# Modulation products in column strips and a first projection that runs inner chunk by inner chunk

## The chip, the cores and the metric

One core of one Trainium2 chip runs the whole program. The metric is device microseconds (us) of one execution; three executions of the kernel before gave 1886.78, 1886.98 and 1887.4, and the median, 1886.98 us, is the time before.

## The reference, cut to what matters

One layer of an encoder is applied to two token streams, x_prompt (1024 tokens) and x_sample (512 tokens), each of width 1024, with the same weights. Each stream has one conditioning vector `c`, which is turned into six modulation vectors of width 1024:

```python
mod = (jnp.dot(jax.nn.silu(c), w_ada) + b_ada)[:, None, :]
sh1, sc1, gt1, sh2, sc2, gt2 = jnp.split(mod, N_MOD, axis=-1)

h = rms_norm(x, g_pre_mix) * (1.0 + sc1) + sh1
proj = jnp.dot(h, w_in)                      # q, k, v of 12 heads, and two gMLP inputs
...                                          # dilated attention in 3 groups, gMLP, concat
mix = jnp.dot(jnp.concatenate([attn, gm], axis=-1), w_out)
x = x + gt1 * rms_norm(mix, g_post_mix)

h = rms_norm(x, g_pre_ffn) * (1.0 + sc2) + sh2
gate, up = jnp.split(jnp.dot(h, w_gu), 2, axis=-1)
f = jnp.dot(jax.nn.silu(gate) * up, w_down)
return x + gt2 * rms_norm(f, g_post_ffn)
```

Nothing of the layer's main work can begin before `sh1` and `sc1` (modulations 0 and 1) are there, because they go into every `h`. The other four modulations are needed later: `gt1` when the first output projection is finished, `sh2` and `sc2` ahead of the FFN, `gt2` at its end.

## The kernel before

**Layout.** Tokens are cut into three groups of 512: groups 0 and 1 are x_prompt (class P, two halves), group 2 is x_sample (class S). Activations lie transposed, 128 channels on the partitions and 512 tokens along the row, in KC = 8 inner chunks. A large product is made by `mm3` (L158): per inner chunk three matmuls, high part by high part, high by low, low by high, with operands that `split` (L137) has cut in two (a ScalarE cast, then a subtraction on VectorE or GpSimd). One output tile of 128 columns for 512 tokens is thus 24 matmuls of 128x512.

**The planner.** The program is written as plain Python in an order; the framework (`schedule_with_timeline_sim=True`, L1054) then orders the instructions of each engine by its own estimate of the time line, with the program order as priority. Buffers belong to tags with a fixed count (`BUFS`, L103; `PBUFS`, L114). The tags that matter here are `tb` (2 buffers of 512 columns), `xc` (3), `h` (16), `wraw` (4), `whl` (4), `sc` (6) and the PSUM tags `st` (2 banks) and `mm` (4 banks).

**The start.** `run` (L937) begins with `ada_first` (L290), a generator of four steps, one per quarter of modulations 0 and 1. A step loads four 512 KB pieces of `w_ada` into `h` buffers and multiplies them with `silu(c)`: the two columns of `silu(c)` lie in a wide field of zeros in two `qk` buffers, and a window that slides over it by 32 columns puts four column blocks into one 128x128 result. That is 32 matmuls of 128x128 a step, each written as two instructions, so 256 instructions in all. VectorE then transposes the result into a `tb` tile and `finish_mod` (L280) adds the bias and makes G, which is (1 + sc1) * g_pre_mix. Between the steps `run` loads group 0, computes its row statistics (`x_stats`, L349, then `rms_now` and `spread`, which use `st` banks and one `tb` tile), loads the weights of two projection tiles (`FIRST_WIN`), and after the fourth step loads group 1. Then `make_h(0)` and `make_h(1)` run one after the other through `modulate` (L374), which makes one chunk of `h` from x: VectorE multiplies x by the row statistics into a `tb` tile (L380), ScalarE applies G and the shift in place (L382), ScalarE casts the high part (L138), and GpSimd (H01 = 'P') subtracts the low part (L139).

**The projections.** `attention_slot` (L680) goes over nine tiles of q, k and v; for class P each tile is made for both halves, by `project` (L407): the weights of a tile are loaded and split, all 24 matmuls of half 0 are issued, evacuated from PSUM, then those of half 1. For the first slot of P the first two tiles are projected together.

**The other modulations.** `ada_rest` (L318) is a generator that `more_ada` (L423) advances by a rate per projected tile, and `ffn` (L894) by one step per pair of hidden tiles. One step handles half of the inner dimension for one block of 512 columns of one modulation: four loads of 256 KB (three into `xc`, one into `tb`), four matmuls with a stationary operand of 32 columns (two real ones, 30 zeros; `silz`) that write to four strips of 32 partitions of one `st` bank, a ScalarE copy of the bank into a `tb` tile (L336), four matmuls with `sel` that add the strips and turn the result (L338), and a copy or an addition into `mod`. Each of these matmuls is written as two instructions. Four modulations times two blocks times two halves make 16 steps.

## Time and profile before

| | us |
|---|---|
| median of three executions | 1886.98 |
| the profiled execution | 1886.02 |
| its span, first to last instruction | 1884.2 |
| TensorE busy (matmul) in the span | 1846.7 |
| VectorE, ScalarE, GpSimd busy | 928.3, 690.6, 149.0 |
| mean granted share of the TensorE clock | 0.993 |

The profile shows one execution. TensorE's instructions appear on two rows, PE (matmul) and PEld (weight load), which overlap. "Idle before" is the time for which an engine waited, and the arrow names what ended the wait. The queue that issues transfers is SP. Times in the timeline count from the first instruction of the span.

### The profile page before, as it was taken

The page shows a single profiled execution, that of the slowest core. Times are in us where ns is not written, and L with a number is a line of the kernel's source. Part 1 is how long each engine was busy: PE and PEld are TensorE (multiplying, and loading weights), DVE is VectorE, ACT ScalarE, POOL GpSimd, SP SyncE. Part 2 cuts the span into 40 slices and gives each one's busy share as a digit, 9 for nine tenths or more (in the row PEclk, how much of TensorE's full clock was granted, in tenths as well). Part 3 has the DMA queues.
Part 4 walks back from the last instruction along what each step waited for, and adds up shares of the span by engine and source line. Part 5 has one row for each costly group of instructions (what it writes and reads, how often), then busy time and mean ns, then how long its engine had stood idle before and what let it go on. Part 6 is the DMA issues. An engine that isn't in the chain of part 4 may idle for free.

```text
span 1884.2 us, 23515 instructions
## 1 busy us (share of the span) xinstructions
PE 1846.7 (98%) x8866; PEld 1471.2 (78%) x8866; DVE 928.3 (49%) x1447; ACT 690.6 (37%) x1180; POOL 149.0 (8%) x102
## 2 busy tenths in 40 slices
PE   7999999999999999999999999999999999999997
PEld 7777876766777777878888888888888888888886
DVE  4334864473795467834443427444442374444223
ACT  3511642152444456533333423333342333333222
POOL 1400100010122012100000100000020000000001
PEclk9999999999999999999999999999999999999999
DMA  8112322234353367642223435322243342222432
GB/s 340 38 55 76 110 95 93 90 118 134 111 176 114 132 218 217 213 162 92 97 94 108 123 94 181 109 95 95 95 122 97 95 169 97 93 95 95 137 96 75
DMA packets 123682, 228.30 MB, mean 121 GB/s; under 512 B 13744, under 2 KB 19120, under 8 KB 123568
## 3 DMA queue, kind: packets, MB, share of 16 engines
q1 hardware_dynamic: 123424, 226.73, 36.2%
q8 instruction: 69, 1.13, 0.2%
q14 instruction: 45, 0.37, 0.1%
q10 hardware_dynamic: 144, 0.07, 0.0%
HBM read 206.30 MB, written 20.45 MB: 120 GB/s over the span
## 4 chain that ended last, share of the span: by engine, by line
PE 59%; DVE 0%; POOL 0%; DVEq 0%; ACT 0%; issue 0%
PE pmm L156 58%; PE pst L156 1%; DVE sc L861 0%; DVE sc L863 0%; POOL rq L216 0%; DVE whl L139 0%; DVEq L1054 0%; ACT tb L227 0%; DVE rq L215 0%
## 5 line engine op out<-in xcount | busy, mean ns | idle before, releaser
L156 PE MATMUL pmm<-h,whl 128*128 128x512 f32 x5772 | 1384.2, 398 | 11.7 <-ACT h L138 5.2
L156 PEld LDWEIGHTS pmm<-h,whl 128*128 128x128 f32 x5772 | 1079.1, 189 | 288.6 <-issue 22.6
L139 DVE TENSOR_TENSOR whl<-wraw,whl 128x512 fp32r<-128x512 f32 (+1 forms) x548 | 386.0, 707 | 461.3 <-ACT whl L138 458.1
L138 ACT CAST whl<-wraw 128x512 fp32r<-128x512 f32 (+1 forms) x548 | 333.2, 609 | 674.4 <-PE pmm L156 558.5
L139 POOL TENSOR_TENSOR h<-tb,h 128x512 fp32r<-128x512 f32 x40 | 59.6, 1497 | 554.9 <-ACT h L138 546.7
L156 PE MATMUL pmm<-qk,whl 128*128 128x512 f32 x414 | 100.0, 394 | 0.0
L908 DVE SCALAR_TENSOR_TENSOR ta<-ta,pmm 128x512 f32<-128x512 f32 x66 | 45.4, 687 | 110.8 <-ACT ta L907 110.7
L156 PEld LDWEIGHTS pmm<-qk,whl 128*128 128x128 f32 x414 | 77.8, 188 | 18.3
L907 ACT ACTIVATE ta<-pmm 128x512 f32<-128x512 f32 x66 | 39.5, 598 | 141.4 <-PE pmm L156 141.4
L909 DVE SCALAR_TENSOR_TENSOR ta<-ta,pmm 128x512 f32<-128x512 f32 x66 | 45.3, 687 | 79.2 <-PE pmm L156 79.0
L190 DVE TENSOR_TENSOR acc<-acc,ta 128x512 f32<-128x512 f32 x55 | 38.6, 702 | 55.4 <-ACT ta L807 44.3
L156 PE MATMUL pst<-qk 64*128 64x128 f32 (+3 forms) x384 | 61.7, 320 | 0.7 <-DVE st L782 0.7
L156 PEld LDWEIGHTS pst<-qk 64*128 64x128 f32 (+1 forms) x384 | 45.6, 187 | 20.1 <-issue 14.3
L216 POOL TENSOR_TENSOR rq<-rq,half 128x4 f32<-128x4 f32 (+1 forms) x11 | 11.7, 1068 | 526.6 <-DVE rq L215 521.9
L382 ACT ACTIVATE tb<-tb,mod,G 128x512 f32<-128x512 f32 x48 | 38.8, 815 | 39.8 <-DVE tb L380 36.0
L156 PE MATMUL pmm<-v,whl 128*128 128x512 f32 x207 | 51.4, 392 | 0.0
L139 POOL TENSOR_TENSOR h<-xc,h 128x512 fp32r<-128x512 f32 x24 | 33.7, 1414 | 171.3 <-ACT h L138 155.1
L806 ACT ACTIVATE sc<-pmm,G 128x512 f32<-128x512 f32 x47 | 32.2, 686 | 40.8 <-PE pmm L156 40.6
L156 PEld LDWEIGHTS pmm<-v,whl 128*128 128x128 f32 x207 | 38.8, 188 | 8.8
L460 DVE SCALAR_TENSOR_TENSOR sc<-cst,pst 128x512 f32<-128x512 f32 (+2 forms) x56 | 26.9, 512 | 37.8 <-PE pst L156 37.7
L620 POOL PARTITION_ALL_REDUCE st<-st x8 | 21.0, 2637 | 224.1 <-DVE st L556 224.1
L156 PE MATMUL pst<-h,qk 128*128 128x128 f32 x256 | 31.8, 286 | 7.0 <-DMA h<-in_wada 6.8
(163 smaller groups left out, 1299.6 us busy)
## 6 DMA issues: line engine op xcount, KB each, us to landing
wraw<-in_wgu SPq DMA_DIRECT2D x264, 256.0 KB, 2.7
wraw<-in_wdn SPq DMA_DIRECT2D x120, 256.0 KB, 2.6
wraw<-in_win SPq DMA_DIRECT2D x84, 256.0 KB, 2.8
xc<-in_wada SPq DMA_DIRECT2D x48, 256.0 KB, 3.7
wraw<-in_wout SPq DMA_DIRECT2D x48, 256.0 KB, 3.0
xc<-in_x SPq DMA_DIRECT2D x40, 256.0 KB, 3.6
xc<-x SPq DMA_DIRECT2D x40, 256.0 KB, 3.7
h<-in_wada SPq DMA_DIRECT2D x16, 512.0 KB, 9.6
```

Of the source, the lines that this page charges most:

```text
L138: self.nc.scalar.copy(hi, src)
L139: (eng or self.nc.vector).tensor_tensor(out=lo, in0=src, in1=hi.bitcast(F32), op=ALU.subtract)
L156: self.nc.tensor.matmul(out, lhsT, rhs, start=start, stop=stop, skip_group_check=True)
L190: nc.vector.tensor_tensor(out=acc, in0=acc, in1=t, op=ALU.add)
L216: nc.gpsimd.tensor_tensor(out=y, in0=y, in1=self.half8[:, :n], op=ALU.pow)
L382: nc.scalar.activation(t, t, AF.Identity, bias=sh[:, kc, c:c + 1], scale=G[:, kc, c:c + 1])
L460: self.nc.vector.scalar_tensor_tensor(out=out, in0=table, scalar=slope, in1=ps, op0=ALU.mult, op1=ALU.add)
L620: self.nc.gpsimd.partition_all_reduce(x[:, :grp.n], x[:, :grp.n], channels=128, reduce_op=RED.max)
L806: nc.scalar.activation(ys[-1][:, mt % 2], ps, AF.Copy, scale=G[:, mt, c:c + 1])
L907: nc.scalar.activation(t, ps[0], AF.Tanh, scale=0.5)
L908: nc.vector.scalar_tensor_tensor(out=t, in0=t, scalar=1.0, in1=ps[0], op0=ALU.add, op1=ALU.mult)
L909: nc.vector.scalar_tensor_tensor(out=t, in0=t, scalar=0.5, in1=ps[1], op0=ALU.mult, op1=ALU.mult)
```

## The change

- `ada_first` multiplies with `silz`: a stationary operand of 32 columns per inner chunk, eight matmuls of 128x512 a step, into four strips of one bank, inner chunks 4 to 7 added onto the strips of 0 to 3. A new helper `turned` copies the bank into a `tb` tile and adds and turns the strips with `sel`, as `ada_rest` did. The layout of the first two modulations' weights in memory changes with it, and the two columns of `sel` are loaded early by a transfer of their own.
- `ada_rest` makes one step out of two: eight loads, eight strip matmuls into one bank, one turn, one copy. The 16 steps become 8, and the rates at which they are called are halved (in `ffn`, every second pair).
- `run` issues group 0's load first, then the first step, group 0's statistics and group 1's load. The rest (three steps, group 1's statistics, `make_h`) moves into `start`, which is called inside the first attention slot behind the weight loads of four tiles.
- The first four tiles of P's first slot go through a new `project_first`: for half 0 the loop over inner chunks is the outer one, with the four tiles inside it and four `mm` banks open; half 1 follows tile by tile as before. The weights of the third and fourth of them lie in `sc` buffers.
- `make_h(0)` and `make_h(1)` are woven, chunk by chunk; the low part of half 0 is made on VectorE (H0 = 'V'), that of half 1 on GpSimd (H1 = 'P').

```diff
+    def turned(self, ps, n):
+        e = self.t2("tb")
+        self.nc.scalar.copy(e, ps)
+        for i in range(n):
+            self.mm(ps[:, 2 * i:2 * i + 2], e[:, 128 * i:128 * i + 128], self.sel, i == 0)
+        return ps[:, 0:2 * n]
+
     def ada_first(self):
-        z = []
-        for i in range(2):
-            t = self.t("qk", [128, 4, 256])
-            nc.vector.memset(t, 0.0)
-            nc.vector.tensor_copy(t[:, :, 96:98], self.sil[:, 4 * i:4 * i + 4])
-            z.append(t)
         for ch in range(4):
             ps = self.p("st")
             for pc in range(4):
-                w = self.t("h", [128, 2, 4, 128])
+                w = self.t("h", [128, 2, 512])
                 nc.sync.dma_start(out=w, in_=self.a["wada1"][ch, pc])
                 for k2 in range(2):
                     kc = 2 * pc + k2
-                    for q in range(4):
-                        self.mm(ps[:, 0:128], z[kc // 4][:, kc % 4, 96 - 32 * q:224 - 32 * q], w[:, k2, q],
-                                kc == 0 and q == 0, kc == 7 and q == 3)
-            tr = self.t2("tb")
-            nc.vector.transpose(out=tr[:, 0:128], in_=ps[:, 0:128])
+                    j = 32 * (kc % 4)
+                    self.mm(ps[j:j + 32], self.silz[:, kc], w[:, k2], kc < 4)
             ks = slice(2 * ch, 2 * ch + 2)
             nc.vector.tensor_copy(self.mod[:, 0:2, ks, :],
-                                  tr[:, 0:128].rearrange("p (m k i) -> p m k i", m=2, k=2)[:, :, :, 0:2])
+                                  self.turned(ps, 4).rearrange("p (m k i) -> p m k i", m=2, k=2))
             self.finish_mod(0, ks)
             self.finish_mod(1, ks)
             yield
 
     def ada_rest(self, ms):
         for m in ms:
             for blk in range(2):
                 ks = slice(4 * blk, 4 * blk + 4)
-                for hf in range(2):
-                    ws = []
-                    for j in range(4):
-                        w = self.t2("xc" if j < 3 else "tb")
-                        nc.sync.dma_start(out=w, in_=self.a["wada2"][m - 2, 4 * hf + j, :, 512 * blk:512 * blk + 512])
-                        ws.append(w)
-                    ps = self.p("st")
-                    for j in range(4):
-                        self.mm(ps[32 * j:32 * j + 32], self.silz[:, 4 * hf + j], ws[j], True)
-                    e = self.t2("tb")
-                    nc.scalar.copy(e, ps)
-                    for i in range(4):
-                        self.mm(ps[:, 2 * i:2 * i + 2], e[:, 128 * i:128 * i + 128], self.sel, i == 0)
-                    o = self.mod[:, m, ks]
-                    pv = v3(ps[:, 0:8], 2)
-                    if hf:
-                        nc.vector.tensor_tensor(out=o, in0=o, in1=pv, op=ALU.add)
-                    else:
-                        nc.vector.tensor_copy(o, pv)
-                    yield
+                ps = self.p("st")
+                for kc in range(KC):
+                    w = self.t2("tb" if kc % 4 == 3 else "xc")
+                    nc.sync.dma_start(out=w, in_=self.a["wada2"][m - 2, kc, :, 512 * blk:512 * blk + 512])
+                    j = 32 * (kc % 4)
+                    self.mm(ps[j:j + 32], self.silz[:, kc], w, kc < 4)
+                nc.vector.tensor_copy(self.mod[:, m, ks], v3(self.turned(ps, 4), 2))
                 self.finish_mod(m, ks)
+                yield
 
+    def project_first(self, grp, tiles, steps):
+        ws = []
+        for i, (ti, _, _) in enumerate(tiles):
+            ws.append(self.weights(self.a["win"][ti], tag="whl" if i < 2 else "sc"))
+        yield
+        ps = [self.p("mm") for _ in tiles]
+        for kc in range(KC):
+            for p, w in zip(ps, ws):
+                o = slice(128 * (kc % 4), 128 * (kc % 4) + 128)
+                hk, wk = self.h[grp.halves[0]][kc], w[kc // 4]
+                self.mm(p, wk[:, 0, o], hk[:, 0], kc == 0, False)
+                self.mm(p, wk[:, 0, o], hk[:, 1], False, False)
+                self.mm(p, wk[:, 1, o], hk[:, 0], False, kc == KC - 1)
+        for hf, gi in enumerate(grp.halves):
+            for i, (w, (_, evac, after)) in enumerate(zip(ws, tiles)):
+                if hf:
+                    ps[i] = self.p("mm")
+                    self.mm3(ps[i], w, range(KC), self.h[gi])
+                self.flush()
+                with self.tc.high_priority(offset=1):
+                    evac(hf, ps[i])
...
         if grp is self.P and sp == 0:
-            tiles[:2] = [tiles[0] + tiles[1]]
+            first = self.project_first(grp, [t[0] for t in tiles[:4]], steps)
+            next(first)
+            start()
+            for _ in first:
+                pass
+            tiles = tiles[4:]
...
-            if j >= 4:
+            if j >= 4 and j % 2 == 0:
                 next(self.ada, None)
...
         ada = self.ada_first()
-        next(ada)
         load = [self.resident(self.a["x"][0], ["st", "st", "qk", "qk"])]
+        nc = self.nc
+        nc.sync.dma_start(out=self.cst[:, 640:642], in_=self.a["cst"][:, 640:642])
         next(ada)
         rs = {0: self.x_stats(load[0])}
-        next(ada)
-        for ti in FIRST_WIN:
-            self.ready[ti] = self.weights(self.a["win"][ti], share=SHARE[0])
-        next(ada)
-        load.append(self.resident(self.a["x"][1], ["v", "v", "v", "vm"]))
-        self.back.append(self.make_h(0, rs[0], load[0], H01))
-        self.tick(-1)
-        self.nc.sync.dma_start(out=self.cst[:, 128:], in_=self.a["cst"][:, 128:])
-        self.nc.sync.dma_start(out=self.row, in_=self.a["row"])
-        self.back.append(self.make_h(1, self.x_stats(load[1]), load[1], H01))
-        self.tick(-1)
-        self.ada = self.ada_rest((2, 3, 4))
+        load.append(self.resident(self.a["x"][1], ["v", "v", "v", "sc"]))
+
+        def start():
+            next(ada)
+            rs[1] = self.x_stats(load[1])
+            next(ada)
+            next(ada)
+            self.back.append(weave(self.make_h(0, rs[0], load[0], H0), self.make_h(1, rs[1], load[1], H1)))
+            self.tick(-1)
+            nc.sync.dma_start(out=self.cst[:, 128:640], in_=self.a["cst"][:, 128:640])
+            nc.sync.dma_start(out=self.row, in_=self.a["row"])
+            self.ada = self.ada_rest((2, 3, 4))
...
-RATE = (0.6, 0.4, 0.5, 1)
+RATE = (0.3, 0.2, 0.25, 1)
-FIRST_WIN = (2, 5)
-H01 = 'P'
+H0 = 'V'
+H1 = 'P'
```

## Rows read from the trace of the kernel before

**Rows 1.** Page, parts 1 and 4: busy time, share, instructions; chain by engine.
```profile
PE 1846.7 (98%) x8866; PEld 1471.2 (78%) x8866; DVE 928.3 (49%) x1447; ACT 690.6 (37%) x1180; POOL 149.0 (8%) x102
PE 59%; DVE 0%; POOL 0%; DVEq 0%; ACT 0%; issue 0%
```

**Rows 2.** Busy time by stretch: stretch us, engines (count), PEclk, DMA share, GB/s.
```profile
0.00:10.00 10.00, 5.12 (x30) 5.16 (x31) 2.62 (x8) 1.50 (x2) 0.41 (x7) 1.00 0.79 288
10.00:20.00 10.00, 8.07 (x72) 7.88 (x71) 5.49 (x16) 4.60 (x8) 0.89 (x1) 1.00 1.03 415
...
30.00:40.00 10.00, 9.86 (x89) 9.67 (x87) 3.77 (x13) 4.08 (x7) 0.00 (x0) 1.00 1.03 408
...
42.70:53.00 10.30, 8.65 (x24) 6.72 (x25) 5.57 (x10) 6.61 (x10) 9.73 (x6) 0.51 0.01 4
53.00:60.00 7.00, 7.00 (x36) 5.81 (x34) 1.39 (x2) 4.59 (x9) 4.24 (x4) 1.00 0.00 0
```

**Rows 3.** PE groups, stretches 40:74.5 (first row) and 74.58:103.1 (others).
```profile
L156 PE MATMUL pmm<-h,whl 128*128 128x512 f32 x76 | 24.1, 475 | 5.5 <-ACT h L138 4.6 <-POOL h L139 0.8
...
L156 PE MATMUL pmm<-h,whl 128*128 128x512 f32 x116 | 28.0, 397 | 0.3 <-DVE whl L139 0.3
L549 PE MATMUL pst<-cst,vm 128*128 128x128 f32 x12 | 1.9, 278 | 0.0
```

**Rows 4.** Timeline, 28 to 43 us: start, us, engine, line, operation, count.
```profile
28.11 0.58 ACT L232 COPY rs<-pst 128x512 f32<-128x512 f32 x1
...
36.31 2.28 DVE L190 TENSOR_TENSOR acc<-acc,ta 128x512 f32<-128x512 f32 x3 [2.43 <-ACT ta L354]
...
39.90 0.32 DVE L310 STREAM_TRANSPOSE tb<-pst 128x128 f32<-128x128 f32 x1 [1.30 <-PE pst L156]
40.14 0.65 DVE L380 TENSOR_TENSOR tb<-st,rs 128x512 f32<-128x512 f32 x1
...
42.72 1.22 PE L156 MATMUL pmm<-h,whl 128*128 128x512 f32 x2 [2.86 <-ACT h L138]
```

**Rows 5.** Timeline, 45 to 50 us: one chunk of h, and the next in its buffer.
```profile
45.44 0.68 DVE L380 TENSOR_TENSOR tb<-st,rs 128x512 f32<-128x512 f32 x1
...
46.15 0.81 ACT L382 ACTIVATE tb<-tb,mod,G 128x512 f32<-128x512 f32 x1 [1.58 <-DVE tb L380]
...
47.00 0.62 ACT L138 CAST h<-tb 128x512 fp32r<-128x512 f32 x1
...
47.69 1.41 POOL L139 TENSOR_TENSOR h<-tb,h 128x512 fp32r<-128x512 f32 x1 [0.45 <-ACT h L138]
...
49.14 0.69 DVE L380 TENSOR_TENSOR tb<-qk,rs 128x512 f32<-128x512 f32 x1 [1.10 <-POOL h L139]
```

**Rows 6.** Page, part 5: the subtraction of the low part on VectorE.
```profile
L139 DVE TENSOR_TENSOR whl<-wraw,whl 128x512 fp32r<-128x512 f32 (+1 forms) x548 | 386.0, 707 | 461.3 <-ACT whl L138 458.1
```

**Rows 7.** PE timeline: first step of ada_rest, its strips, matmuls behind, its turn.
```profile
103.12 0.63 PE L156 MATMUL pst<-xc,silz 128*32 128x512 f32 x3
...
104.12 5.38 PE L156 MATMUL pmm<-h,whl 128*128 128x512 f32 x22
109.34 0.95 PE L156 MATMUL pst<-cst,tb 128*128 128x2 f32 x8
110.15 0.48 PE L156 MATMUL pmm<-h,whl 128*128 128x512 f32 x1
```

**Rows 8.** PE timeline: a strip that runs alone (its two instructions), and what follows.
```profile
286.95 1.04 PE L156 MATMUL pst<-xc,silz 128*32 128x512 f32 x2
287.93 0.74 PE L156 MATMUL pmm<-h,whl 128*128 128x512 f32 x2
```

**Rows 9.** SP and PE timeline: a load of ada_rest's ninth step, and its strip.
```profile
409.93 0.37 SPq L330 DMA_DIRECT2D xc<-in_wada  x1
...
416.30 1.05 PE L156 MATMUL pst<-xc,silz 128*32 128x512 f32 x2
```

**Rows 10.** Page, part 6: loads of ada_rest, count, KB, median us to landing.
```profile
xc<-in_wada SPq DMA_DIRECT2D x48, 256.0 KB, 3.7
```

More of the change, by code (lines that the diff above doesn't have):

```diff
@@ L419, in project @@
                 if hf == len(grp.halves) - 1:
+                    self.pending.append(after)
+        self.more_ada(len(tiles) * RATE[grp.c])
+    def project_first(self, grp, tiles, steps):
[19 more added lines that the diff above has]
+                    evac(hf, ps[i])
+                if hf:
+                    self.tick(steps)
                     self.pending.append(after)
@@ L678, in values, with attention_slot @@
             yield
-    def attention_slot(self, grp, sp, steps, between=None):
+    def attention_slot(self, grp, sp, steps, between=None, start=None):
         sc = [{}, {}]
@@ L963, in run @@
                 self.alongside(self.x_stats_behind(self.chunks(self.a["x"][2]), rs, 2))
-            self.attention_slot(self.P, sp, STEPS[0], next_group if sp else None)
+            self.attention_slot(self.P, sp, STEPS[0], next_group if sp else None, None if sp else start)
             if not sp:
@@ L1020, in lay_out @@
     wa = f("w_ada")[0].reshape(KC, 128, 6, KC, 128)
-    w1 = wa[:, :, 0:2].reshape(4, 2, 128, 2, 4, 2, 4, 32)
-    a["wada1"] = w1.transpose(4, 0, 2, 1, 6, 3, 5, 7).reshape(4, 4, 128, 2, 4, 128)
+    w1 = wa[:, :, 0:2].reshape(4, 2, 128, 2, 4, 256)
+    a["wada1"] = w1.transpose(4, 0, 2, 1, 3, 5).reshape(4, 4, 128, 2, 512)
     a["wada2"] = wa[:, :, 2:6].reshape(KC, 128, 4, D).transpose(2, 0, 1, 3)
```

## The prediction

> **What bounds the kernel now.** I read the busy shares and the chain of waits first: PE is busy for 98% of the span and it alone makes up the chain [rows 1]. So a time changes in two ways only: PE gets more or less to do, or PE stands or crawls less. The second can only be found where it now does so, so next come the stretches of the first 75 us and the PE groups in them. Until 40 us the transfers are what is full: 415 to 408 GB/s in the three stretches from 10 to 40 us [rows 2]. From 40 to 74.5 us PE makes 76 matmuls of 128x512, at a mean of 475 ns, and waits 5.5 us, nearly all of it for a chunk of h [rows 3]; for ten of these us its granted clock is 0.51, that is, the lower of its two levels (1.2 GHz) [rows 2]. In the steady stream 22 such matmuls take 5.22 us from the first start to the next instruction's [rows 7], 0.237 us each. By that price 76 are 18.0 us; the stretch took 34.5. From 74.5 to 103.1 us the stream is dense: 116 matmuls (27.5 us by the price) and 12 transposes in 28.5 us [rows 3]. After that the kernel is PE work, so a change there is worth what it adds to or takes from PE's queue.
>
> The sum is made against the profiled execution, 1886.02 us (its span of 1884.2 and 1.8 around it); the median is 1.0 above it, and I take the differences off the median. About 0.2%, 3.8 us, is what a measurement here can tell from no change.
>
> **Part 1, the first modulations in strips.** Half of the 256 small matmuls run back to back up to 39.9 us, where the last VectorE transpose ends them [rows 4], so PE set the end of this phase together with the transfers. The strips are far less work: a step is four groups like the one that took 1.00 us [rows 7]. But now the transfers set the end: the 16 pieces (8.4 MB), both x loads (4.2 MB) and the eight weight loads of four tiles (2.1 MB) make 14.7 MB; by the rates of [rows 2] 2.9 MB are in at 10 us and some 4.1 more every 10 us, 15.2 at 40, so 14.7 MB are in at 38.7 us. If the planner puts the last four weight loads (1.05 MB) behind the pieces, because their `wraw` buffers are not free yet, the last piece is in at 36.1. I take 37.5. Hence the step's gain on PE is mostly hidden by the loads, and it is priced by where it leaves the first projection.
>
> **Part 2, does h follow its chunks?** The diff reads as if chunks 0 and 1 of h could be made as soon as the first step is done. I think they can't. In the kernel before, the first multiplication of `make_h` (L380) needed only x and the row statistics, copied at 28.1 us, and one of two `tb` buffers. VectorE did three additions for group 1, which come later in the program and wait for later data, ahead of it, and took it up right behind the last step's transpose, 40.14 after 39.90 [rows 4]. That is what a planner does that hands out the buffers of a tag in program order: the fourth step's `tb` tile stood ahead of h's. In the changed program the fourth step's tile (in `turned`) stands ahead of h's as well. So ScalarE takes up h only behind the copy of the fourth step: last piece 37.5, its last strips 1.5 (at the lower clock; 1.0 at the full one [rows 7]), a PSUM copy 0.6 (priced by the copy of the statistics [rows 4]), scale and shift 0.81, cast 0.62 [rows 5], some 0.3 for handing over: the first projection matmul at 41.3 us, with 39.9 and 43.5 as bounds (pieces in at 36.1, or at 38.7 with a slower end). It is at 42.72 now [rows 4].
>
> **Part 3, four tiles inside the chunk loop.** Here is the gain. A chunk of h holds its `tb` buffer from 45.44 to 49.14, 3.70 us, of which 1.41 is the subtraction on GpSimd [rows 5]; on VectorE it is 0.71 [rows 6], so 3.00. With two buffers, a chunk of half 0 and one of half 1 are made every 3.35 us at best. The other bound is the pace that half 0 had before: four chunks from 40.14 [rows 4] to 49.14 [rows 5], 4.5 us a pair. Group 1's additions ran among those, and they have moved ahead of the pieces, so I take 3.6, near the lower bound. In these 3.6 us PE now has 12 matmuls, 2.84 us, where before it had six of two tiles and waited. Chunk 7 is cast seven pairs behind chunk 0, at 41.3 + 25.2 = 66.5, and its 12 matmuls end half 0 at 69.4: 96 matmuls done. Before, 76 were done at 74.5, and the 96th 20 x 0.237 = 4.7 later, at 79.2. Half 1 then streams, its chunks are made by the same time, and PE goes on as it now does. That is 9.8 earlier; the four transposes that before are also done by then (0.16 us each by [rows 3], 0.6) come off: **9 us gained**. Bounds: 39.9 with 3.35 gives 66.3 (12 gained), 43.5 with 4.5 gives 77.9 (1 gained). Group 1's loads move ahead of the pieces too (counted above); the weight splits of two more tiles (ScalarE 0.62 [rows 5], VectorE 0.71 [rows 6], four times each) fall into time in which both engines wait for transfers, and cost up to 2.5 us of ScalarE if their loads come last, inside the bounds.
>
> At a lower clock a chunk's 12 matmuls take up to 5.7 us. The strips occupy PE thinly before 41 us, so it starts at the lower level, as it does now at 42.7 [rows 2]. The Trainium skill ("TensorE: Matmul & The Clock Gate", section "Loop structure matters more than you think") speaks against this change: a loop that waits for data between short matmul bursts runs cold. This trace agrees for 42.7 to 53.0, clock 0.51, and shows no paced stretch as dense as the new one. If the level were low only for the first two chunks, PE would fall some 4 us behind h and make it up at 0.8 a chunk, ending at most 1 us later.
>
> **Part 4, the other modulations.** A strip group of four costs 1.00 us of PE's queue (103.12 to 104.12) and a turn 0.81 (109.34 to 110.15) [rows 7]. A strip that runs alone costs 0.98 (286.95 to 287.93), as much as four together [rows 8]. Of the 16 steps, 13 ran their four together, two ran them in three parts and one in four: 23 parts, 22.6 us. With 16 turns (0.84 on average) it is 36.1 us. After, there are eight turns, 6.7 us saved, and at least 16 parts. The second four chunks of a step are the unknown: their `xc` buffers are the first four's, so their loads start only when those strips are done, a load lands in 3.7 us [rows 10], and the planner decides whether the strips run together. Together: 16 parts, 13.5 us saved. One ahead and three together: 24 parts, 5.7 saved. All alone: 40 parts, 10 us lost. Where loads came late before, strips ran alone; where they lay ready, together. I take the middle, **5.7 saved**. ScalarE's and VectorE's half as many copies cost or bring nothing, as neither is on the chain.
>
> Sum: 1886.98 - 9 - 5.7 = **1872.3 us**. Own range 1861 to 1886.
>
> **The rivals.**
>
> (a) *h does follow its chunks.* If `tb` is handed out by need, chunks 0 to 5 are made and multiplied while the later pieces load, and only chunks 6 and 7 wait: modulation ready about 44, two chunks of each half 1.4 us of ScalarE each, two times 2.84 on PE: 96 matmuls done at about 51.5, 27 us gained, 1854 in all. For it speaks that the shape of the change asks for it; against it [rows 4].
>
> (b) *Slower: PE waits in every step of `ada_rest` for its second four chunks.* If the planner sets strips 4 to 7 right behind 0 to 3, PE, which takes its queue in order, stands until loads land that start only then, and the projection matmuls behind stand too. A step then costs 1.00 + w + 0.98 + 0.84 against 4.5 now, with w up to 4.2 (3.7 to land, the rest to issue and to follow one another): 8 x 2.5 = 20 lost, 1886.98 + 20 - 9 = 1898. It makes the change slower by over 0.2% from w = 3.3. Against it: where a strip followed a late load before, the planner left 6.4 us of PE work between them (409.93 to 416.30, matched by their order) [rows 9], more than the landing.
>
> (c) *All second strips alone:* 1886.98 - 9 + 10 = 1888, no change that can be measured.
>
> (d) *The clock stays low through the paced stretch,* the skill's rule as a result: 96 matmuls at twice 0.237 from 41.3 end at 86.8, 7.6 later than now, 1886.98 + 7.6 - 5.7 = 1889. Against it: at the low level the 12 matmuls leave no gap, and before, a full queue at the low level was followed by a granted clock of 1.00 from 53 us on [rows 2].
>
> **How the numbers follow.** Forecast 0.63, (a) 0.13, (b) 0.10, (c) 0.10, (d) 0.04. Faster: nearly all of the forecast's share (0.58) and (a), 0.71. Within 0.2%: the forecast's upper end, most of (c) and (d), 0.16. Slower: (b) and the rest, 0.13. The range takes in (a)'s upper half and (c): 1855 to 1889.
>
> **What would show it.** ScalarE's first scale and shift behind the fourth step's copy, near 40 us, bears out part 2; one at 20 us is (a). The 96th projection matmul near 69 us bears out part 3. Strips 4 to 7 in groups or alone, and 64 turn instructions of `ada_rest` instead of 128, decide part 4; PE waits on loads of `in_wada` behind 100 us are (b). The granted clock from 45 to 70 us decides (d). I am wrong most easily in the pace of the pairs (3.6) and the parts per step (3).

## The result, and the profile after

| | before | after |
|---|---|---|
| device time, median | 1887.19 us | 1899.36 us |
| range of the runs | 1885.94 to 1892.64 | 1896.70 to 1901.76 |
| ratio, 95% interval | | 1.0061 [1.0046, 1.0076] |
| profiled execution, its span | 1886.02, 1884.2 | 1900.29, 1898.5 |

The change makes the kernel 12 us slower, where 15 us less had been forecast: outside the range, and on the other side. The start was gained about as forecast; the other modulations lost more than that.

Busy time of PE and VectorE and the chain of waits of the kernel after (page, parts 1 and 4), to be held against [rows 1]:

```profile
PE 1854.0 (98%) x8642; PEld 1443.8 (76%) x8642; DVE 930.1 (49%) x1439; ACT 689.5 (36%) x1176; POOL 136.1 (7%) x94
PE 87%; DVE 4%; DMA 4%; issue 2%; POOL 1%; ACT 1%; SPq 0%; DVEq 0%; POOLq 0%; ACTq 0%
```

PE has 224 instructions fewer and is busy 7.3 us longer. Its idle time (the span less its busy time) grows too, from 37.5 to 44.5 us, but 5.4 of these 7.0 us lie in the first 100 us, where the strips leave PE less to do and the kernel is ahead; from 100 to 880 us it is 1.5. So behind the start the loss is for the most part not waiting: PE's work itself became dearer.

The start after, first by stretch (columns as in [rows 2]), then single rows of its timeline (as in [rows 4]):

```profile
40.00:50.00 10.00, 7.64 (x33) 4.79 (x26) 8.36 (x24) 7.98 (x13) 1.91 (x2) 0.83 0.43 150
50.00:60.00 10.00, 8.79 (x35) 6.07 (x34) 6.09 (x9) 7.06 (x11) 3.36 (x3) 1.00 0.12 43
```

```profile
40.72 0.58 ACT L293 COPY tb<-pst 128x512 f32<-128x512 f32 x1 [2.25 <-PE pst L156]
41.35 0.81 ACT L368 ACTIVATE tb<-tb,mod,G 128x512 f32<-128x512 f32 x1
...
42.86 0.93 PE L156 MATMUL pmm<-h,whl 128*128 128x512 f32 x2 [0.45 <-ACT h L138]
...
59.22 0.73 PE L156 MATMUL pmm<-h,whl 128*128 128x512 f32 x2
...
62.82 0.73 PE L156 MATMUL pmm<-h,whl 128*128 128x512 f32 x2
...
66.41 0.74 PE L156 MATMUL pmm<-h,whl 128*128 128x512 f32 x2
...
70.01 0.73 PE L156 MATMUL pmm<-h,whl 128*128 128x512 f32 x2
...
73.31 11.09 PE L156 MATMUL pmm<-h,whl 128*128 128x512 f32 x47
...
97.42 2.95 PE L156 MATMUL pmm<-h,whl 128*128 128x512 f32 x12
```

The fourth step's copy is followed by the first scale and shift of h, then come chunks every 3.6 us, and half 0's 96 matmuls are done at 73.3. The 192nd is done at 97.4, against 103.1 before [rows 7]: PE is 5.7 us ahead when the steady stream begins.

That lead is lost again, and 14 us with it, nearly all between 160 and 870 us. The first step of `ada_rest` after, PE's timeline:

```profile
160.33 0.63 PE L156 MATMUL pst<-xc,silz 128*32 128x512 f32 x3
...
161.33 3.05 PE L156 MATMUL pmm<-h,whl 128*128 128x512 f32 x12
...
168.38 1.05 PE L156 MATMUL pst<-xc,silz 128*32 128x512 f32 x2
...
169.79 1.04 PE L156 MATMUL pst<-xc,silz 128*32 128x512 f32 x2
...
172.12 0.62 PE L156 MATMUL pst<-xc,silz 128*32 128x512 f32 x1
...
177.29 0.95 PE L156 MATMUL pst<-cst,tb 128*128 128x2 f32 x8
```

The first four strips run together (1.00 us to the next start), then the fifth alone (0.97), the sixth alone (0.97), the last two together (0.98). Each part costs the same, however many strips are in it, as in [rows 7, 8]. Over all eight steps the strips run in 37 parts; before, the 64 strips of 16 steps ran in 23. And from 160 to 178 us one `st` bank is held by a half-finished sum. What that does to the scores is seen in two stretches of the timelines, after and before:

```profile
359.72 0.48 PE L156 MATMUL pst<-qk 64*128 64x128 f32 x2
360.13 0.73 PE L156 MATMUL pmm<-h,whl 128*128 128x512 f32 x2
360.80 0.48 PE L156 MATMUL pst<-qk 64*128 64x128 f32 x2
```

```profile
364.53 1.16 PE L156 MATMUL pst<-qk 64*128 64x128 f32 x8
365.61 1.05 PE L156 MATMUL pst<-cst,tb 128*128 128x2 f32 x8
...
371.35 1.71 PE L156 MATMUL pst<-qk 64*128 64x128 f32 x16
372.99 2.36 PE L156 MATMUL pmm<-h,whl 128*128 128x512 f32 x9
```

A score product has 64 rows (one head's operands lie on partitions 0 to 63, the other's on 64 to 127) and is written as two instructions; eight of them are one head's four products. The price is again by the run and not by the instruction: eight in one run take 1.08 us to the next start and sixteen (both heads, in part side by side) 1.64, but two that stand alone take 0.41, so that eight in four runs take 1.64. The projections between such runs become dearer too: two take 0.67 (360.13 to 360.80), where the dense stream takes 0.47. Counted in the traces from 100 to 880 us, the 288 score instructions stand in 54 runs before and in 71 after. The Trainium skill (page "TensorEngine Tiling (Array Packing)", section "Restrictions and Gotchas") says that tiles of different rows write to different PSUM banks, so that row tiling raises the need for banks. These traces agree, but it is the smaller part: 51 score instructions before and 40 after start within 0.02 us of the one ahead of them, as two heads side by side would.

Summed over 100 to 880 us, where all of `ada_rest` lies first before, then after. Three rows of each are groups of instructions (busy us, mean ns of one, idle time before them); the fourth is the strips alone (stretch, us, PE busy and count, granted clock, DMA share, GB/s):

```profile
L156 PE MATMUL pmm<-h,whl 128*128 128x512 f32 x2341 | 578.7, 401 | 6.0 <-DVE whl L139 3.9 <-DVE h L139 1.4 <-ACT h L138 0.6
L156 PE MATMUL pst<-qk 64*128 64x128 f32 (+3 forms) x384 | 61.7, 320 | 0.7 <-DVE st L782 0.7
L156 PE MATMUL pst<-cst,tb 128*128 128x2 f32 x128 | 15.7, 245 | 0.0
100.00:880.00 780.00, 24.32 (x128) 1.00 0.39 131
```

```profile
L156 PE MATMUL pmm<-h,whl 128*128 128x512 f32 x2261 | 566.6, 403 | 8.8 <-DVE whl L139 7.8 <-ACT h L138 0.6 <-ACT whl L138 0.2
L156 PE MATMUL pst<-qk 64*128 64x128 f32 (+3 forms) x384 | 68.0, 324 | 1.2 <-DVE qk L139 1.2
L156 PE MATMUL pst<-cst,tb 128*128 128x2 f32 x64 | 7.8, 244 | 0.0
100.00:880.00 780.00, 38.86 (x128) 0.99 0.39 129
```

Strips 24.3 to 38.9, turns 15.7 to 7.8: +6.7 us. Scores 61.7 to 68.0: +6.3 (96 of the 384 instructions in that row are other products, whose time hardly changes). Waits of the projections 6.0 to 8.8: +2.8 (those for split weights rise from 3.9 to 7.8, those for h fall from 2.0 to 0.6). That is 15.8 of the 20.0 us between a lead of 5.7 and a lag of 14.3 at the end (the spans).

Most of the rest may be the clock. After, the granted clock is 0.57, 0.58 and 0.57 in the stretches from 200 to 204, 545 to 549 and 736 to 740 us, each of them shortly behind a wait of PE of 1.2 to 2.1 us; before, it is so only from 725 to 729 (0.57), behind a wait of 1.97. Four us at 0.57 lose about 1.7, so that two such stretches more are some 3.4 us, an estimate.

### The profile page after: what moved, and what is told of

The parts are those of the page before. It is cut to its first block, busy times and chain, and to the rows that moved or that the text cites. A ratio compares the mean times of both kernels' runs of the same rounds, so it can differ in the third digit from the quotient of the medians.

```text
span 1898.5 us, 23006 instructions
## 1 busy us (share of the span) xinstructions
PE 1854.0 (98%) x8642; PEld 1443.8 (76%) x8642; DVE 930.1 (49%) x1439; ACT 689.5 (36%) x1176; POOL 136.1 (7%) x94
## 4 chain that ended last, share of the span: by engine, by line
PE 87%; DVE 4%; DMA 4%; issue 2%; POOL 1%; ACT 1%; SPq 0%; DVEq 0%; POOLq 0%; ACTq 0%
PE pmm L156 79%; PE pst L156 6%; PE ppv L156 2%; DMA xc<-rden 2%; DMA h<-in_wada 1%; DVE sc L598 1%; DVE whl L139 1%; POOL h L139 1%; DVE sd L598 0%; DVE sc L837 0%; DMA wraw<-in_win 0%; DMA xc<-in_x 0%; DVE xc L889 0%; DVE sc L879 0%; PE pst L562 0%
## 5 line engine op out<-in xcount | busy, mean ns | idle before, releaser
L156 PE MATMUL pmm<-h,whl 128*128 128x512 f32 x5676 | 1367.4, 398 | 11.8 <-DVE whl L139 7.8
L156 PEld LDWEIGHTS pmm<-h,whl 128*128 128x128 f32 x5676 | 1059.8, 189 | 297.5 <-issue 33.0
L156 PEld LDWEIGHTS pmm<-qk,whl 128*128 128x128 f32 x414 | 77.8, 188 | 18.4
L139 POOL TENSOR_TENSOR h<-tb,h 128x512 fp32r<-128x512 f32 x32 | 46.2, 1447 | 552.0 <-ACT h L138 543.8
L156 PE MATMUL pst<-qk 64*128 64x128 f32 (+3 forms) x384 | 68.0, 324 | 1.2 <-DVE qk L139 1.2
L156 PE MATMUL pst<-xc,silz 128*32 128x512 f32 x96 | 38.8, 605 | 0.0
```

Source lines behind the costliest of these rows:

```text
L139: (eng or self.nc.vector).tensor_tensor(out=lo, in0=src, in1=hi.bitcast(F32), op=ALU.subtract)
L156: self.nc.tensor.matmul(out, lhsT, rhs, start=start, stop=stop, skip_group_check=True)
```

## The experiments

Each time stands against runs of the kernel before on the same chip at the same time, so ratios are compared. Nothing of the computation is left out in any of these kernels.

### The change in its parts

The new start (`ada_first` in strips, `project_first`, woven h) with the old `ada_rest` and its rates:

```diff
-                ps = self.p("st")
-                for kc in range(KC):
...
+                for hf in range(2):
... (ada_rest as before)
-RATE = (0.3, 0.2, 0.25, 1)
+RATE = (0.6, 0.4, 0.5, 1)
```

> The changed start (strips in ada_first, project_first, woven h) with ada_rest and its rates as before the change. Theory: the start is a gain of about 5.7 us (the 192nd projection matmul at 97.4 instead of 103.1) and everything that is lost is lost by ada_rest, so 1881.5 us, ratio 0.997, with 23 strip parts behind 100 us and the score matmuls in pairs of heads again. Rival: the new start shifts the later work against ada_rest's loads and that is the loss; then most of it stays, 1892 us or more, ratio above 1.002.

Measured: 1879.99 us, ratio 0.9957 [0.9944, 0.9969]. The start alone is worth 7.9 us.

The reverse, the old start with the new `ada_rest`:

> The start as before the change, with the new ada_rest and its rates alone. Theory: ada_rest's own instructions cost 7 us more (37 parts at 0.98 and 8 turns instead of 23 and 16), and the bank it holds costs some 12 more in the score matmuls and around them: 1906 us, ratio 1.010. Rival: only ada_rest's own instructions count: 1894 us, ratio 1.0037.

Measured: 1903.03 us, ratio 1.0078 [1.0064, 1.0092]. The strips are busy 38.86 us and the scores 67.9, as in the kernel after. So the new `ada_rest` costs 15 us with the old start. The two effects add up to +7, and after is at +12: some 4 to 5 us arise only with both together. By the intervals of the three ratios this is 4.9 with about 4.5 to either side, so barely clear of noise. The clock may be a part of it: between 100 us and the last 13 us, the profiled execution of the start alone has no stretch at the lower clock, that of the new `ada_rest` alone has one, and the kernel after has three. No run here decides it.

Column strips in `ada_first` alone, everything else as before:

```diff
-                    for q in range(4):
-                        self.mm(ps[:, 0:128], z[kc // 4][:, kc % 4, 96 - 32 * q:224 - 32 * q], w[:, k2, q],
-                                kc == 0 and q == 0, kc == 7 and q == 3)
+                    j = 32 * (kc % 4)
+                    self.mm(ps[j:j + 32], self.silz[:, kc], w[:, k2], kc < 4)
```

> The kernel before, with the first modulations in column strips and nothing else of the change (the load order, the projections and ada_rest stay). Theory A: PE ended this phase before, and with strips the transfers do; the fourth step's pieces are then preceded by only 11.6 MB, which are in at about 31 us, so the first projection matmul comes near 36 us instead of 42.7 and the paced stretch behind it moves as a whole: 1881 us, ratio 0.9965, no less than the whole new start brings. Theory B, that of the prediction: the gain is in the four tiles inside the chunk loop, and the paced stretch is bound by how fast h is made and by group 1's load, so strips alone bring 0 to 2 us: 1886 us.

Measured: 1882.20 us, ratio 0.9970 [0.9961, 0.9980]; the first projection matmul comes at 38.95 instead of 42.72 [rows 4], the 96th at 77.8 instead of 79.2. The time is near theory A's, but its mechanism did not occur: the paced stretch does not move as a whole, and of the 3.8 us at the first matmul 1.4 are left at the 96th, as h sets the pace between them (the granted clock is 0.67 and 0.66 from 40 to 50 and from 60 to 70 us). Where the other 3 of the 4.6 us come from is not shown; the profiled execution, 1883.75 us, is the second slowest of the twelve. The strips alone thus bring more than half of what the whole new start brings (0.9957).

### The other modulations

The bank of `ada_rest` taken from the projections' tag, in the kernel after:

```diff
-                ps = self.p("st")
+                ps = self.p("mm")
```

> The changed kernel, with the result of an ada_rest step in a bank of the tag mm (4 banks) instead of st (2 banks). Theory: the strips still run apart (36 parts, 7 us more than before), but the score matmuls find both of their banks and run in pairs of heads; 6 to 9 of the 12 us that are lost beside the strips come back: 1891 us, ratio 1.002. Rival: the bank does not matter and the loss beside the strips comes from elsewhere: 1899 us, ratio 1.006.

Measured: 1901.31 us, ratio 1.0070 [1.0057, 1.0082], no better than after, so the theory's 1891 is excluded. The scores did fall (61.3 us), so the rival, by which the bank does not matter, is not borne out either. The profiled execution was the slowest of the five, with its first projection matmul at 46.6, 3.7 later than after's. The same edit with the old start:

> The old start with the new way of the other modulations, their PSUM bank taken from the projections' tag mm instead of the scores' tag st. The kernel with this way alone stood at 1903.0 (15.2 over before); in its trace the scores take 67.9 us against 61.7 before, and strips and turns 6.7 more. Theory (the held st bank costs some 6 us, and these come off the total when the bank is another's): scores near 61.5, time 1897 (10 over before). Rival (what the scores get back, the projections lose, since the bank that is held is now one of theirs): scores near 61.5, but 1901 or more.

Measured: 1900.71 us, ratio 1.0070 [1.0053, 1.0088], against 1.0078 [1.0064, 1.0092] with the bank of the scores: between the two expectations, and not to be told from no difference. Groups of 100 to 880 us in this kernel:

```profile
L156 PE MATMUL pst<-qk 64*128 64x128 f32 (+3 forms) x384 | 60.2, 325 | 1.1 <-DVE qk L139 1.0
L156 PE MATMUL pmm<-xc,silz 128*32 128x512 f32 x96 | 38.8, 605 | 2.9 <-DMA xc<-in_wada 2.9
```

The scores get 7.7 us back, and 2.9 of it go into waits of strips for their loads, which had not been there. So the held bank is the cause of the dearer scores, but the total gains at most a few us from giving it to another tag. That the projections, which are now one bank short, take back the rest is not shown: their waits are 6.9 us here and 8.3 with the bank of the scores.

Next the cause of the parts. In the changed kernel the second four loads of a step need the buffers of the first four. Steps of 256 columns over the whole inner dimension have eight half-sized chunks, and all eight fit into the four buffers:

```diff
-            for blk in range(2):
-                ks = slice(4 * blk, 4 * blk + 4)
+            for qt in range(4):
+                ks = slice(2 * qt, 2 * qt + 2)
+                ws = []
+                for j in range(4):
+                    w = self.t2("xc" if j < 3 else "tb")
+                    for r in range(2):
+                        nc.sync.dma_start(out=w[:, 256 * r:256 * r + 256],
+                                          in_=self.a["wada2"][m - 2, j + 4 * r, :, 256 * qt:256 * qt + 256])
+                    ws.append(w)
...
-                    w = self.t2("tb" if kc % 4 == 3 else "xc")
...
+                    self.mm(ps[32 * j:32 * j + 32, 0:256], self.silz[:, kc], ws[j][:, 256 * r:256 * r + 256], kc < 4)
...
-RATE = (0.3, 0.2, 0.25, 1)
+RATE = (0.6, 0.4, 0.5, 1)
```

> The changed kernel, with ada_rest in 16 steps of 256 columns over the whole inner dimension: eight half-size chunks fit in the four buffers, so all eight strips are loaded ahead, run together, and the bank is held as briefly as before the change. Theory: a step is 1.0 for eight strips of half the length and 0.42 for half a turn, 16 times 1.42 = 22.7 and some 2 for steps that are still split, against 36.1 before, and the start's 5.7 come on top: 1887.2 - 5.7 - 11.4 = 1870 us, ratio 0.991. Rival: strips and turns of half the size cost as much as whole ones (their weights bound them): 16 times 1.84, no gain beside the start's, 1881 us, ratio 0.997.

Measured: 1875.87 us, ratio 0.9937 [0.9923, 0.9951], 23.5 us below after, midway between the two expectations, with the sum still made over the whole inner dimension. One step in its timeline:

```profile
162.47 0.42 PE L156 MATMUL pst<-xc,silz 128*32 128x256 f32 x3
...
163.14 0.39 PE L156 MATMUL pst<-xc,silz 128*32 128x256 f32 x3
...
168.74 0.61 PE L156 MATMUL pst<-cst,tb 128*128 128x2 f32 x4
```

All eight strips of this step stand in one run, as they do in 11 of the 16 steps, and the turn is half as long. The same step in the kernel before, with nothing else changed and one load for each buffer:

> The kernel before with the other modulations alone changed, to sixteen steps of 256 columns over the whole inner dimension, the same 16 places in the projections. Theory (16 steps x (2 groups of 4 half strips at about 0.5 + a turn of 2 pairs, 0.42) = 23 us against 36.1 before, less a part for strips that come in parts): 4 to 8 us gained, 1879 to 1883. Rival (the strips' time is hidden or given back to waits for a bank, so that only the sum over the whole inner dimension, not its place, matters): 1886 or more.

Measured: 1877.96 us, ratio 0.9950 [0.9935, 0.9965], 9.7 us gained, more than either expectation. Its rows of 100 to 880 us:

```profile
L156 PE MATMUL pst<-qk 64*128 64x128 f32 (+3 forms) x384 | 63.3, 321 | 0.0
L156 PE MATMUL pst<-cst,tb 128*128 128x2 f32 x64 | 8.4, 237 | 0.0
100.00:880.00 780.00, 22.85 (x256) 1.00 0.41 133
```

Against the rows of before: strips 1.5 less, turns 7.3 less, scores 1.6 more, 7.2 in all of the 9.7. So summing over the inner dimension in PSUM does pay what it saves in turns, if a step's chunks all have a buffer. The loss of the change is the missing buffers, not the sum. (A step of 512 columns with eight buffers was not run; this is read from the narrower one.) With the new start the narrower step gains less than these 9.7 us: 4 against the start alone (0.9957 to 0.9937, intervals that overlap).

### The start

The tiles that `turned` and the row statistics take from `tb` moved to `xc` until h begins, in the kernel with the new start alone:

```diff
+        self.early = "xc"
...
-        dg = self.t2("tb")
+        dg = self.t2(self.early)
...
-        e = self.t2("tb")
+        e = self.t2(self.early)
...
+            self.early = "tb"
             self.back.append(weave(self.make_h(0, rs[0], load[0], H0), self.make_h(1, rs[1], load[1], H1)))
```

> The kernel of e1_start_only (new start, ada_rest as before), with the copies of the four steps and the diagonals of the two statistics in xc buffers instead of tb buffers, until make_h begins. Theory: tb was handed out in program order, and that kept h behind the fourth step; with xc the chunks 0 to 5 of h are made while the pieces load, ScalarE's first scale and shift comes near 25 us instead of 41, the 96th projection matmul near 61 instead of 70 to 73: 11 us less than e1_start_only, 1869 us, ratio 0.990. Rival: h waits for the pieces or for ScalarE anyway: like e1_start_only, 1880 us.

Measured: 1883.81 us, ratio 0.9983 [0.9975, 0.9992]: both expectations missed, and slower than with `tb` (0.9957) by 0.26%, 5 us. ScalarE in that kernel:

```profile
24.89 0.80 ACT L383 ACTIVATE tb<-tb,mod,G 128x512 f32<-128x512 f32 x1
...
39.04 0.58 ACT L233 COPY rs<-pst 128x512 f32<-128x512 f32 x1 [0.97 <-PE pst L157]
40.39 0.81 ACT L383 ACTIVATE tb<-tb,mod,G 128x512 f32<-128x512 f32 x1 [0.76 <-DVE tb L381]
```

The first chunk of h is made at 24.89 instead of 41.35, with three of the four steps still to come: the queue in front of it was that of `tb`, handed out in program order. But the second chunk waits until 40.39, behind the copy of group 1's statistics at 39.04. In the woven order the next tile of `tb` belongs to half 1, and half 1 needs those statistics. One queue was opened and the next one stood behind it. So the weaving was undone, in the kernel with the new start alone:

```diff
-            self.back.append(weave(self.make_h(0, rs[0], load[0], H0), self.make_h(1, rs[1], load[1], H1)))
+            for i in range(2):
+                self.back.append(self.make_h(i, rs[i], load[i], "VP"))
```

> The kernel of e1_start_only, with the chunks of half 0 all made ahead of those of half 1, their low parts on VectorE and GpSimd by turns, instead of woven. Theory: woven, a pair takes 3.5 us and PE has 2.84 us to do in it; unwoven a chunk takes 1.7 and PE is full from the first chunk on: 96 projection matmuls done near 67 us instead of 73, and half 1's chunks are just in time: 1875 us, ratio 0.993. Rival: half 1 then waits for its chunks and gives all of it back: 1880 us.

Measured: 1873.75 us, ratio 0.9928 [0.9913, 0.9943], some 6 us below the woven one; half 0 ends at 69.3. The edit does a second thing: with "VP" the low parts of each half are made on VectorE and GpSimd by turns, where half 0's had all been made on VectorE. No run separates the two. From 50 us on PE has no gap:

```profile
50.00:60.00 10.00, 10.00 (x45) 8.04 (x44) 7.41 (x10) 7.21 (x12) 2.60 (x2) 1.00 0.23 79
60.00:70.00 10.00, 10.00 (x44) 8.04 (x43) 5.41 (x9) 8.34 (x14) 3.89 (x3) 1.00 0.01 2
```

The same edit in the changed kernel itself:

> The changed kernel with one edit: the two halves of h made one after the other instead of woven. Theory (the woven order lets half 0 have only every second tile of tb, so that PE stands in the paced stretch; it has nothing to do with the other modulations): the 6.2 us that the same edit gave to the kernel with the new start alone come off here too, 96th projection matmul by 69.5, time 1893. Rival (the other modulations or their loads then stand earlier against the projections and take it back): 1897 or more.

Measured: 1893.12 us, ratio 1.0027 [1.0016, 1.0039]; 96 matmuls are done at 68.9. The 6 us come with this edit, whatever the other modulations do.

Both queues opened, in the kernel with the new start alone:

> The new start with the old way of the other modulations, the turning and table tiles of the start in xc instead of tb, and the two halves of h made one after the other instead of woven. Theory (two buffer queues stand between the pieces and the projections: the program order of tb, and inside it the alternation of the two halves): with both gone, h of the first half follows its pieces from about 25 us, the 48 products with the whl tiles are done by about 47 us when the sc tiles arrive, the other 48 take 11.4 us at 0.237, so the 96th projection matmul ends near 60 (69.3 in the unwoven kernel, 76.8 in the xc kernel), the 192nd near 83, and the time is 1864 (10 below the unwoven kernel). Rival (a third queue, the ScalarE and VectorE work or the late loads of the sc tiles, holds the first 96 anyway): 96th at 68 or later, time 1872 or more.

Measured: 1877.45 us, ratio 0.9944 [0.9930, 0.9957]: the rival's side, and no better than the unwoven kernel (0.9928). The first projection matmul is at 27.87, yet the 96th is at 71. Its timeline, ScalarE and then PE:

```profile
44.55 0.58 ACT L294 COPY xc<-pst 128x512 f32<-128x512 f32 x1
49.64 1.52 ACT L383 ACTIVATE tb<-tb,mod,G 128x512 f32<-128x512 f32 x2 [4.51 <-DVE G L288]
51.57 0.57 ACT L294 COPY xc<-pst 128x512 f32<-128x512 f32 x1
```

```profile
46.29 1.66 PE L157 MATMUL pmm<-h,whl 128*128 128x512 f32 x6
47.79 0.95 PE L157 MATMUL pst<-cst,xc 128*128 128x2 f32 x8
...
49.71 1.06 PE L157 MATMUL pst<-h,silz 128*32 128x512 f32 x8
```

The third step's bank is copied at 44.55, but its turn stands on PE behind projection matmuls and starts at 47.79; the fourth step's last strips follow at 49.71 and its copy at 51.57, 10.9 us later than after's. PE takes its queue in order, and projection matmuls that wait for h now stand in front of the strips that the next h needs. That this is the third queue is read from the rows; no run here moves the strips forward.

### The parts put together

The step of 256 columns with the start's tiles in `xc` (woven), then without them but unwoven, then with both:

> The kernel of e4_quarters (each buffer filled by one load instead of two, from a layout made for it), with the xc buffers of e6_start_xc at the start. Theory: the two gains add up, 1876 - 11 = 1865 us, ratio 0.988. Rival: what the start gains is given back where the steps of ada_rest meet other work: 1872 us or more.

Measured: 1875.79 us, ratio 0.9941 [0.9926, 0.9955], the rival's side: no better than the step of 256 columns without these tiles (0.9937).

> The new start, h unwoven, and the other modulations in sixteen steps of 256 columns over the whole inner dimension, one load per buffer. Theory (the strips were dear only since they came alone and held their bank; eight half loads that fit in four buffers keep them together): the 4.1 us between the quarters kernel (1875.9) and the kernel with the new start alone (1880.0) come on top of the unwoven kernel's 1873.75: 1869.5. Rival (both take the same idle time, or the halves' order changes which queue is late): 1873 or more.

Measured: 1869.57 us, ratio 0.9898 [0.9882, 0.9914]. This is the best of all, 18 us below the kernel before in its own comparison, and where the theory had put it.

> Both of the other two kernels' edits together: start's tiles in xc, h unwoven, modulations in sixteen steps. Theory: 1864 less 4 us, 1860. Rival (xc buffers given to the start make the first sixteen-step loads late, or the start is held elsewhere): 1868 or more.

Measured: 1871.58 us, ratio 0.9908 [0.9892, 0.9923]. Again the rival's side: the tiles in `xc` bring nothing here either.

## Why the prediction was wrong, step by step

**What bounds the kernel.** Right: PE's queue sets the time in both traces, and what the change cost is found in PE's own work. It follows that a step that saves instructions can still lose, and that is where I went wrong.

**Part 1, the strips of the first modulations.** Nearly right in time. The fourth step's last strips start at 39.53 and its copy at 40.72, where I had 39.0 for the end of the strips. It was not the transfers that ended last: PE waits for pieces 11.9 us in all, in two waits, the longer one (11.0) before its first instruction. What came last was the order of copy, turn and strips of the third and fourth steps on PE and ScalarE.

**Part 2, h does not follow its chunks.** Right, and shown. The first scale and shift follows the fourth step's copy (41.35 behind 40.72), and moving those tiles to another tag brought it to 24.89. The first projection matmul came at 42.86 instead of 41.3, inside the bounds. Rival (a) would not have come true by that alone: two more queues stand behind the first, the weaving (shown) and PE's own order (read from rows).

**Part 3, four tiles in the chunk loop.** The mechanism was right, a term was off. From 59.22 on, the pair pace is 3.60, 3.59 and 3.60 us, as assumed. But chunk 0 starts 1.6 late, and the seven pairs take 27.2 us instead of 25.2 (42.86 to 70.01), as the first ones share ScalarE and VectorE with the splitting of the third and fourth tiles' weights and run at a granted clock of 0.83. I had put that at nothing to 2.5, inside the bounds. Half 0 ends at 73.3 instead of 69.4: 5.7 us gained where I took 9. The start alone, run by itself, was worth 7.9 in the median. What I did not ask is whether the paced stretch had to be paced: the weaving gives half 0 only every second `tb` tile, and without it, and with the low parts by turns on two engines, the same PE work has no gap (6 us).

**Part 4, the other modulations.** This is the step that failed, in two places. First, the term "parts per step": I took three (24 in all) as the middle between 16 and 40; it was 37, near the far end. At the price of [rows 8] 37 parts and eight turns are 37 x 0.98 + 6.7 = 43.0 us against 36.1, 6.9 lost, which is the 6.7 of the rows. The prices were right, the count was not. I had written that strips ran alone where their loads came late, and that the second four loads can only start when the first strips are done; together these say that they come late in every step, and the middle was no fair choice. Second, a cost that the prediction does not have: the step holds its `st` bank from the first strips to the end of the turn, 18 us in the first step instead of 7 [rows 7], and the scores, which share the tag, break into more runs and lose 6.3 us. Nor did I price the 2.8 us that the projections wait longer, or the clock.

**The rivals.** (b) has a time close to the result (1898), but its mechanism did not occur. The waits of PE behind 100 us:

```profile
PE pmm L156 <- DVE whl L139: 7.8, 6, 2.1
PE pst L156 <- ACT tb L227: 3.0, 1, 3.0
```

None is for a load of `in_wada`: the strips were set 7 us apart, as [rows 9] had led me to expect, and other work filled the gap. The price was paid in parts, which is (c)'s mechanism; (c) gave 1888 since it had neither the bank nor the waits nor the smaller gain of the start. (d) did not come: the granted clock is 0.83 from 40 to 50 us and 1.00 from 50 to 60, in a paced stretch in which PE is busy for 8.79 of 10 us. So the rule on loop structure (the Trainium skill, "TensorE: Matmul & The Clock Gate", section "Loop structure matters more than you think") had no price in this stretch. Further on the clock did fall three times, shortly behind waits of 1.2 to 2.1 us, and that may have cost some 3.4 us more than before.

**The sum.** Forecast: 9 gained in the start, 5.7 in the modulations. Measured with one part each: 7.9 gained and 15.2 lost, and 4 to 5 more lost when both are there (barely clear of noise). Nearly all of the error is part 4.

## What to carry to other kernels

A sum that is kept open in PSUM over more chunks than there are buffers saves evacuations but breaks its matmuls into parts and holds its bank while the missing loads come; count the buffers first, and shrink the chunk until a whole sum fits (here 256 columns instead of 512: with the old start, 15 us lost became 10 us gained). Where small matmuls on different strips run side by side, price them by the run and not by the instruction, and ask who else uses the bank that they hold. Where one queue in program order is opened, look for the next one before pricing the gain: buffers of a tag, the alternation of two producers, and the order of an engine stood behind each other here, and opening only the first made that kernel slower.

## What was not expected of the hardware

Two score instructions take 0.41 us to the next start, eight in one run 1.08, sixteen of both heads, in part side by side, 1.64: 0.21, 0.14 and 0.10 for each. In the run of eight the first and the last take 0.21 and 0.20 to the next start and those between them 0.11. What a PSUM bank that is held elsewhere costs thus shows in the trace only as a different grouping of the same instructions.

The column of the granted clock did not always tell the level at which instructions ran. The same turn of eight instructions, in the kernel after:

```profile
19.00 1.87 PE L156 MATMUL pst<-cst,tb 128*128 128x2 f32 x8 [0.69 <-ACT tb L293]
...
33.85 1.05 PE L156 MATMUL pst<-cst,tb 128*128 128x2 f32 x8 [0.69 <-ACT tb L293]
```

The column reads 1.00 in all three stretches from 10 to 40 us, yet the turn takes 1.87 at 19.00 and 1.05 at 33.85, and the eight matmuls that spread the row statistics take 2.05 at 20.73 and 1.14 at 34.77. Until 11 us PE had done nothing. The trace of this execution holds no record of the clock before 33.0 us, and a stretch without a record reads 1.00. The kernel with the new start alone has records from 17.4 us on, and there durations and clock agree: the turn takes 1.05 at 18.54, 1.87 at 33.19 (granted clock 0.50 from 21 to 37 us) and 1.05 at 40.06 (1.00 from 38 to 44). So early in this program the durations of a repeated instruction are the better sign.
